# One-core attention and feed-forward layer: an unused load dropped, two weight loads moved ahead of two others, a bias product repeated, all engines' order rewritten

## Chip, core and metric

The kernel runs on one core of one Trainium2 chip. The metric is the device time of one execution in microseconds (us), the median of several runs. Before the change it is 332.9 us (three runs, 332.89 to 332.98).

## What is computed

The reference is one transformer layer on 256 tokens of width 1024 in float32. One wide projection is split into sixteen parts for four mixers; their outputs are joined, projected back, and followed by a feed-forward part.

```python
h = x @ w_in                                   # 256 x 1024 @ 1024 x 2956
(q_n, kc, vc, ks, vs, kw, vw, g_n, q_m, k_m, v_m, conv_in, q_h, f_h, i_h, g_h) = split(h)
kc = gelu(blocks(kc) @ w1[0] + b1[0]) @ w2[0]  # compressor, 15 blocks of 32 tokens; vc the same
o_nsa  = nsa_attention(q_n, kc, vc, ks, vs, kw, vw, sigmoid(g_n), rel_tab[:4])
o_moba = moba_attention(q_m, k_m, v_m, rel_tab[4:])
o_conv = silu(layer_norm(depthwise_conv31(a * sigmoid(g)) + b)) @ w_pw
o_hgrn = hgrn2(q_h, f_h, i_h, g_h)             # gated linear recurrence, chunks of 64
x = layer_norm(alpha * x + concat(o_nsa, o_moba, o_conv, o_hgrn) @ w_out)
x = layer_norm(alpha * x + square(relu(x @ w_ff1)) @ w_ff2)
```

## The kernel before

**Products.** Float32 products are made of parts: a weight is loaded raw, ScalarE rounds it to a high piece in the format fp32r (L245), VectorE subtracts to get the low piece (L246), and TensorE adds three products: high by high, high by low, low by high (L313 to L315, or L335 to L337 where the weight is the stationary side). The weights of ca, cg, qn and km are used raw in plain float32 (L310, L520). Names of the parts: ca and cg are the convolution's two inputs, n (n1) the keys and compressor inputs of NSA, qn its queries, ni (two halves, ni0 and ni1) the values, gates and HGRN's i, f, q and g those of HGRN, qm, km and vm those of MoBA, w1a and w1b the compressor's two weight matrices in two halves of 1 MB each.

**Loads.** SyncE's queue carries all weights, in the order of the list LOADS, into a pool `raws` of five slots of 1 MB. A transfer is issued when its slot is free, which is when the piece that was there has been rounded, subtracted or multiplied for the last time; behind it in the queue nothing is issued before. ScalarE's high pieces and VectorE's low pieces have three slots each (`his`, `los`), freed by the last product that reads them.

**Stages.** In order of time: the projections ca, cg, n, qn (8 to 33 us), ni (33.5 to 43.5), the compressor's products with w1a (L686), q and f together, score products of NSA (`tt` <- ksw, qn, L371) that VectorE empties with the bias table (L374) and ScalarE turns into weights p (L377, L388), transposes of p (L397), g, vm, qm, km, the four mixers, the product with w_out (L990 to L992) for two token tiles of 128, the first layer norm with its transposes by a product with a scaled identity (L1044, L1051), then the feed-forward part in sixteen groups, from about 146 us to the end. VectorE also does the convolution: 62 operations, one a tap and half (L571, L573), which stand wherever the order puts them, and HGRN's running sum, the scan (L616).

**First layer norm.** Each token tile t has two banks of transposed output, filled by a bias product (L1048, `acc` or `hg` <- bhot, bsum, 40 x 128 by 40 x 512) and four transposes each. The transposes wait for the tile's scale (L1044), at the end of a chain on VectorE that starts when w_out's banks of this tile are complete.

**Order.** Nothing is left to a scheduler at run time: the table ISSUE holds for PE, DVE, Activation, Pool and SP the order of every instruction, as indices into the program's own order, and `issue_in` makes each engine follow it. Each engine takes its instructions strictly in that order.

**Where the change touches it.** LOADS (L184), `load_w1` (L419 to L426), `tapw` (L488, L489), a tile in the space that `mixl` takes later, filled from the input `taps`; the branch CONV_T of `part_conv`, which does not run since CONV_T is empty; the bias product (L1048); ISSUE (L69 to L143).

Of the kernel before, what the change touches and what calls it, by code (L numbers as in the profile page):

```python
# [17 lines left out]
P = 128  # L18
S = 256
# [27 lines left out]
def shape_constants():  # L47
# [13 lines left out]
    for i, b in enumerate(LEVELS):  # L61
# [48 lines left out]
    ),  # L110
    DVE=(
# [13 lines left out]
    ),  # L125
    Activation=(
# [9 lines left out]
    ),  # L136
# [1080 lines left out]
```

## Time and profile before

| | |
|---|---|
| median of the runs | 332.9 us |
| profiled execution, its own time | 335.78 us |
| its span, from the first to the last instruction | 334.0 us |
| mean granted clock of TensorE | 0.986 |
| TensorE busy | 319.8 us (96%) |
| VectorE busy | 233.3 us (70%) |
| ScalarE busy | 166.8 us (50%) |

The profiled execution is 2.9 us above the median; the trace's times are those of this execution. PE is TensorE, DVE VectorE, ACT ScalarE, SP SyncE. A share over the whole span mixes the front (to 146 us, many short pieces on all engines) with the feed-forward part (TensorE in one stream). Where a wait ends is read from the timeline and the chain, and what cost a clock had from the windows.

### The profile page before, as it was taken

How to read it: one execution, taken by the hardware profiler on the slowest of the kernel's cores; microseconds unless marked ns; L12 is line 12 of the kernel's file. 1: busy time of each engine (PE TensorE's matmuls, PEld its weight loads, DVE VectorE, ACT ScalarE, POOL GpSimd, SP SyncE). 2: the span in 40 equal slices, each digit the busy share in tenths (PEclk: the TensorE clock that was granted, in tenths of full speed). 3: DMA queues.
4: the chain of work that ended last, by engine and by line, in shares of the span. 5: the costliest groups of instructions: out<-in, count | busy, mean ns of one | idle time of the engine just before them, and what ended most of it. 6: DMA issues, size and time to landing. Idle time of an engine off the chain costs nothing.

```text
span 334.0 us, 4992 instructions
## 1 busy us (share of the span) xinstructions
PE 319.8 (96%) x1929; PEld 273.1 (82%) x1929; DVE 233.3 (70%) x428; ACT 166.8 (50%) x307; POOL 10.5 (3%) x33
## 2 busy tenths in 40 slices
PE   8999969999999999989999999999999999999990
PEld 6897859898988778788888888888888888888880
DVE  0269969999989866886677477747564756568286
ACT  1464444784899982344365354535453545373100
POOL 3500000000000100000000000100000000000000
PEclk9999998999999999999999999999999999999996
DMA  7999799094300216556567555965565646520012
GB/s 234 387 398 416 235 395 388 15 371 135 121 0 2 54 74 251 153 226 186 214 232 251 176 203 155 318 202 207 153 226 160 219 144 233 156 98 0 2 49 77
DMA packets 18359, 62.75 MB, mean 188 GB/s; under 512 B 1784, under 2 KB 3664, under 8 KB 17696
## 3 DMA queue, kind: packets, MB, share of 16 engines
q1 hardware_dynamic: 15648, 56.61, 47.8%
q0 software_dynamic: 1056, 3.72, 3.2%
q10 hardware_dynamic: 1632, 2.11, 2.2%
q8 instruction: 15, 0.25, 0.3%
q14 instruction: 8, 0.07, 0.1%
HBM read 61.37 MB, written 1.06 MB: 187 GB/s over the span
## 4 chain that ended last, share of the span: by engine, by line
PE 86%; DVE 8%; DMA 2%; ACT 1%; issue 1%; DVEq 0%; ACTq 0%
PE mm L1102 15%; PE mm L1100 8%; PE hg L1121 5%; PE hg L1122 4%; PE tt L1122 4%; PE tt L1120 4%; PE hg L1120 4%; PE tt L1121 4%; DMA w_q_raw<-in_w_in_dram 2%; PE mm_km L310 2%; PE mm L1099 2%; PE mm_cg L310 2%; DVE yc L573 2%; PE acc L292 1%; PE tt L371 1%; PE tt L397 1%
## 5 line engine op out<-in xcount | busy, mean ns | idle before, releaser
L1102 PE MATMUL mm<-x1s,w_hi 128*128 128x512 f32 x210 | 74.4, 394 | 0.0
L246 DVE TENSOR_TENSOR r_lo<-r_raw,r_hi 128x1024 fp32r<-128x1024 f32 x40 | 47.4, 1221 | 24.8 <-ACT r_hi L245 24.8
L1100 PE MATMUL mm<-x1s,w_lo 128*128 128x256 f32 x240 | 61.0, 279 | 0.0
L245 ACT ACTIVATE r_hi<-r_raw 128x1024 fp32r<-128x1024 f32 x40 | 40.6, 1050 | 33.5 <-PE tt L1122 32.4
L1100 PEld LDWEIGHTS mm<-x1s,w_lo 128*128 128x128 f32 x240 | 44.9, 188 | 2.7
L1102 PEld LDWEIGHTS mm<-x1s,w_hi 128*128 128x128 f32 x210 | 39.2, 188 | 7.4
L246 DVE TENSOR_TENSOR w_lo<-w_raw,w_hi 128x1024 fp32r<-128x1024 f32 x32 | 37.8, 1218 | 5.0 <-ACT w_hi L245 5.0
L245 ACT ACTIVATE w_hi<-w_raw 128x1024 fp32r<-128x1024 f32 x32 | 32.2, 1051 | 4.6 <-DMA w_raw<-in_w_ff_dram 4.5
L1106 ACT ACTIVATE fx<-mm 128x256 f32<-128x256 f32 x30 | 11.4, 383 | 44.4 <-PE mm L1102 44.4
L1107 DVE TENSOR_TENSOR fs<-mm,fx 128x256 f32<-128x256 f32 x30 | 12.6, 424 | 28.5 <-ACT fx L1106 28.5
L573 DVE SCALAR_TENSOR_TENSOR yc<-hc,cols,yc 128x256 f32<-128x256 f32 x60 | 27.5, 479 | 0.5
L1121 PE MATMUL hg<-r_lo,fh 128*128 128x512 f32 (+1 forms) x70 | 26.4, 378 | 0.0
L1120 PE MATMUL hg<-r_hi,fh 128*128 128x512 f32 (+1 forms) x70 | 26.4, 377 | 0.0
L1121 PE MATMUL tt<-r_lo,fh 128*128 128x512 f32 x64 | 24.1, 396 | 0.0
L1122 PE MATMUL hg<-r_hi,fl 128*128 128x512 f32 (+1 forms) x70 | 22.4, 376 | 0.0
L1122 PE MATMUL tt<-r_hi,fl 128*128 128x512 f32 x64 | 20.8, 397 | 0.0
L1120 PE MATMUL tt<-r_hi,fh 128*128 128x512 f32 x64 | 20.8, 396 | 0.0
L1121 PEld LDWEIGHTS hg<-r_lo,fh 128*128 128x128 f32 x70 | 13.2, 189 | 2.7
L1122 PEld LDWEIGHTS hg<-r_hi,fl 128*128 128x128 f32 x70 | 13.2, 189 | 2.6
L1120 PEld LDWEIGHTS hg<-r_hi,fh 128*128 128x128 f32 x70 | 13.2, 188 | 2.1
L1121 PEld LDWEIGHTS tt<-r_lo,fh 128*128 128x128 f32 x64 | 12.1, 188 | 2.9
L1122 PEld LDWEIGHTS tt<-r_hi,fl 128*128 128x128 f32 x64 | 12.1, 189 | 2.8
(331 smaller groups left out, 650.7 us busy)
## 6 DMA issues: line engine op xcount, KB each, us to landing
w_raw<-in_w_ff_dram SPq DMA_DIRECT2D x32, 512.0 KB, 4.4
r_raw<-in_w_ff_dram SPq DMA_DIRECT2D x16, 1024.0 KB, 4.9
w<-in_nsa_cmp_w_dram SPq DMA_DIRECT2D x4, 1024.0 KB, 7.6
r_raw<-in_w_out_dram SPq DMA_DIRECT2D x4, 1024.0 KB, 6.1
w_ni_raw<-in_w_in_dram SPq DMA_DIRECT2D x2, 792.0 KB, 11.4
xf<-in_xt_dram ACTq DMA_DIRECT2D x4, 256.0 KB, 6.9
w_ca_raw<-in_w_in_dram SPq DMA_DIRECT2D x4, 256.0 KB, 7.1
w_cg_raw<-in_w_in_dram SPq DMA_DIRECT2D x2, 512.0 KB, 5.8
```

The lines of the kernel that those rows point to most:

```text
L245: A.activation(self.h[:, i:j], self.raw[:, i:j], AF.Copy)
L246: self.last = V.tensor_tensor(self.l[:, i:j], self.raw[:, i:j], self.h[:, i:j].bitcast(F32), op=ALU.subtract)
L310: T.matmul(dst[:, i], w.raw[:, k, P * i:P * i + P], xf[:, k], start=(k == 0), stop=(k == KT - 1))
L573: V.scalar_tensor_tensor(yc[:, i], h, w, yc[:, i], op0=ALU.mult, op1=ALU.add)
L1099: T.matmul(flat(pf[i]), h, flat(x1s[:, k]), start=True, stop=False)
L1100: T.matmul(pf[i][:, 0], l, x1h[:, k], start=False, stop=False)
L1102: T.matmul(flat(pf[i]), h, flat(x1s[:, k]), start=False, stop=(k == KT - 1))
L1106: A.activation(lo[:, i], pf[i][:, 1], AF.Copy)
L1107: V.tensor_tensor(sq[:, i], pf[i][:, 0], lo[:, i], op=ALU.add)
L1120: T.matmul(bank_, h, w.h[:, i, sl], start=(g == 0 and i == 0), stop=False)
L1121: T.matmul(bank_, h, w.l[:, i, sl], start=False, stop=False)
L1122: last = T.matmul(bank_, l, w.h[:, i, sl], start=False, stop=(g == NG - 1 and i == 1 and sl.stop != 768))
```

## The change

It does four things. The input `taps` and its load of 1 MB are dropped, with the branch that would have read it; the 62 taps on VectorE stay. In LOADS q stands before w1a and w1b before g, and w1a's first half goes to the space of `mixl` instead of a slot of `raws`; its load stands right behind qn's in SP's table. The last bias product (tile 1, second bank) is issued six times: five times as a product by itself, whose result the next overwrites, then as before. All five tables are new.

```diff
-    CONV_T = ()
-
-    LOADS = "ca cg n1 ni0 qn f ni1 qm w1a q km g w1b vm".split()
+    LOADS = "ca cg n1 ni0 qn f ni1 qm q w1a km w1b g vm".split()
...
         for i in range(2):
-            raw = raws.tile([P, 2048], F32, name="w1", tag="raw").rearrange("p (a b) -> p a b", a=8)
+
+            pool, tag = (raws, "raw") if c or i else (wk, "mixl")
+            raw = pool.tile([P, 2048], F32, name="w1", tag=tag).rearrange("p (a b) -> p a b", a=8)
             nc.sync.dma_start(raw, I["nsa_cmp_w1"][:, c, i])
...
-    tapw = wk.tile([P, 8, 8, 32], F32, name="tapw", tag="mixl")
-    late(tapw, I["taps"])
...
     def part_conv():
-        nonlocal pcv, yc
+        nonlocal yc
         at_(K["taps"])
         yc = t2_("c", "yc")
-        if CONV_T:
...
         for c in range(2):
-            T.matmul(pts[t][c], bsum, bhot[:, 4 * c:4 * c + 4, None].to_broadcast([40, 4, P]), start=True, stop=False)
+            to = pts[t][c], bsum, bhot[:, 4 * c:4 * c + 4, None].to_broadcast([40, 4, P])
+
+            for _ in range(5 if (t, c) == (1, 1) else 0):
+                T.matmul(*to, start=True, stop=True)
+            T.matmul(*to, start=True, stop=False)
...
     SP=(
-        "0-10 30 28-29 11-27 31-89 "
+        "0-10 18 30 28-29 11-17 19-27 31-89 "
     ),
```

What the tables do is seen in the order of the instructions. First SyncE's queue from f to vm (w_150 and w_152 are the halves of w1a, w_175 and w_177 those of w1b), before:

```order
L228 DMA w_f_raw<-in_w_in_dram 128x1024 x2
L228 DMA w_ni_raw<-in_w_in_dram 128x1584
L228 DMA w_qm_raw<-in_w_in_dram 128x1024 x2
L424 DMA w_150<-in_nsa_cmp_w_dram 128x2048
L424 DMA w_152<-in_nsa_cmp_w_dram 128x2048
L228 DMA w_q_raw<-in_w_in_dram 128x1024 x2
L228 DMA w_km_raw<-in_w_in_dram 128x1024 x2
L228 DMA w_g_raw<-in_w_in_dram 128x1024 x2
L424 DMA w_175<-in_nsa_cmp_w_dram 128x2048
L424 DMA w_177<-in_nsa_cmp_w_dram 128x2048
L228 DMA w_vm_raw<-in_w_in_dram 128x1024 x2
```

and after, from behind qn to w1b (w_159 and w_161 are the halves of w1a, w_166 and w_168 those of w1b):

```order
L424 DMA w_159<-in_nsa_cmp_w_dram 128x2048
L905 DMA pw<-in_conv_pw_w_dram 128x2x256
L665 DMA w_685<-in_nsa_cmp_w_dram 128x128
L667 DMA w2k<-in_nsa_cmp_w_dram 128x256
L226 DMA w_f_raw<-in_w_in_dram 128x1024 x2
L226 DMA w_ni_raw<-in_w_in_dram 128x1584
L226 DMA w_qm_raw<-in_w_in_dram 128x1024 x2
L226 DMA w_q_raw<-in_w_in_dram 128x1024 x2
L424 DMA w_161<-in_nsa_cmp_w_dram 128x2048
L226 DMA w_km_raw<-in_w_in_dram 128x1024 x2
L424 DMA w_166<-in_nsa_cmp_w_dram 128x2048
L424 DMA w_168<-in_nsa_cmp_w_dram 128x2048
```

w1a's first half went ahead of f, ni and qm, its second half behind q; w1b went ahead of g, which follows it, and vm follows g.

Next TensorE behind the last product of ni, where w1a's products (w_150 and w_152) end and those of q begin, before:

```order
L686 MATMUL acc<-w_150,blk_333 32x256
L686 MATMUL acc<-w_152,blk_334 32x256
L371 MATMUL tt<-ksw_329,qn 128x128
L371 MATMUL tt<-ksw_328,qn 128x128
L313 MATMUL mm_q<-xs,w_q_hi 128x256
L314 MATMUL mm_q<-xs,w_q_hi 128x256
L313 MATMUL mm_f<-xs,w_f_hi 128x256
L314 MATMUL mm_f<-xs,w_f_hi 128x256
L315 MATMUL mm_f<-xs,w_f_lo 128x256
```

and after (w_159 and w_161):

```order
L661 MATMUL acc<-w_159,blk_331 32x256
L661 MATMUL acc<-w_161,blk_332 32x256
L661 MATMUL acc<-w_159,blk_331 32x256
L311 MATMUL mm_q<-xs,w_q_hi 128x256
L311 MATMUL mm_f<-xs,w_f_hi 128x256
L312 MATMUL mm_f<-xs,w_f_hi 128x256
L313 MATMUL mm_f<-xs,w_f_lo 128x256
L311 MATMUL mm_f<-xs,w_f_hi 128x256
L312 MATMUL mm_f<-xs,w_f_hi 128x256
```

Both score products stood between w1a's last product and q; now they stand ahead of w1a's first, only nine of its sixteen products come before q, the other seven behind q and f, and a single product of q comes before f's.

Last TensorE at the end of w_out and the first layer norm (scale_1471 and scale_1498 are the scales of token tiles 0 and 1), before:

```order
L992 MATMUL tt<-r_hi,mixl 128x512
L1048 MATMUL acc<-bhot,bsum 128x512 x2
L1048 MATMUL hg<-bhot,bsum 128x512 x2
L1051 MATMUL acc<-scale_1471,x_1341 128x128 x4
L1051 MATMUL hg<-scale_1471,x_1341 128x128 x4
L1051 MATMUL hg<-scale_1498,x_1341 128x128 x4
```

and after (scale_1469 and scale_1496):

```order
L967 MATMUL tt<-r_hi,mixl 128x512
L1027 MATMUL hg<-bhot,bsum 128x512 x2
L1027 MATMUL acc<-bhot,bsum 128x512
L1026 MATMUL acc<-bhot,bsum 128x512 x5
L1027 MATMUL acc<-bhot,bsum 128x512
L1030 MATMUL hg<-scale_1469,x_1339 128x128 x4
L1030 MATMUL acc<-scale_1469,x_1339 128x128 x4
L1030 MATMUL hg<-scale_1496,x_1339 128x128 x4
```

The five extra products stand ahead of tile 0's transposes, with the other bias products; the banks are filled in the opposite order.

## Rows read from the trace of the kernel before

**Rows 1.** The page, part 4: shares of the chain that ended last.

```profile
PE 86%; DVE 8%; DMA 2%; ACT 1%; issue 1%; DVEq 0%; ACTq 0%
```

**Rows 2.** Waits of TensorE: us in total, times, longest.

```profile
PE mm_q L313 <- ACT iv L345: 2.6, 1, 2.6
```

**Rows 3.** Chain that ended last, around 40 us: start, us, what.

```profile
37.27 1.81 DVE w_ni_lo L246
39.10 7.20 DMA w_q_raw<-in_w_in_dram
46.40 1.06 ACT w_q_hi L245
```

**Rows 4.** TensorE's timeline: start, us, what, count [idle before <- releaser].

```profile
43.48 1.93 PE L686 MATMUL acc<-w,blk 128*32 128x256 f32 x32
...
48.39 0.57 PE L313 MATMUL mm_q<-xs,w_q_hi 128*128 128x256 f32 x1 [2.55 <-ACT iv L345]
...
52.04 0.28 PE L314 MATMUL mm_q<-xs,w_q_hi 128*128 128x256 f32 x1
...
52.99 0.28 PE L313 MATMUL mm_f<-xs,w_f_hi 128*128 128x256 f32 x1
```

**Rows 5.** 5 us windows: busy us (count) by engine, PEclk, DMA share, GB/s.

```profile
30.00:35.00 5.00, 4.31 (x22) 3.63 (x21) 4.86 (x13) 4.92 (x7) 0.00 (x0) 1.00 0.95 343
45.00:50.00 5.00, 2.45 (x19) 1.91 (x12) 2.48 (x11) 3.56 (x11) 0.00 (x0) 0.84 1.02 410
50.00:55.00 5.00, 5.00 (x36) 4.49 (x34) 4.39 (x13) 1.49 (x9) 0.00 (x0) 0.81 1.03 420
60.00:65.00 5.00, 5.00 (x61) 4.09 (x59) 4.64 (x13) 3.58 (x5) 0.00 (x0) 1.00 0.01 3
140.00:145.00 5.00, 3.70 (x25) 3.04 (x26) 4.68 (x13) 2.25 (x5) 0.00 (x0) 1.00 0.86 302
```

**Rows 6.** SyncE's queue: start of issue, us, what, count.

```profile
39.10 1.07 SPq L228 DMA_DIRECT2D w_q_raw<-in_w_in_dram  x2
...
52.20 0.80 SPq L228 DMA_DIRECT2D w_vm_raw<-in_w_in_dram  x2
```

**Rows 7.** DMA issues: count, KB each, median us to landing.

```profile
w_raw<-in_w_ff_dram SPq DMA_DIRECT2D x32, 512.0 KB, 4.4
...
tapw<-in_taps_dram POOLq DMA_DIRECT2D x1, 1024.0 KB, 11.2
...
w_km_raw<-in_w_in_dram SPq DMA_DIRECT2D x2, 512.0 KB, 8.6
...
w_vm_raw<-in_w_in_dram SPq DMA_DIRECT2D x2, 512.0 KB, 7.2
```

**Rows 8.** VectorE's timeline from 33 to 50 us.

```profile
33.45 0.41 DVE L595 TENSOR_TENSOR blk<-mm_n,cols 64x240 f32<-64x240 f32 x1
...
40.62 1.67 DVE L573 SCALAR_TENSOR_TENSOR yc<-hc,cols,yc 128x256 f32<-128x256 f32 x4
42.20 2.36 DVE L246 TENSOR_TENSOR w_qm_lo<-w_qm_raw,w_qm_hi 128x1024 fp32r<-128x1024 f32 x2
...
48.97 0.28 DVE L374 CUSTOM_DVE_ANT_0 p<-tt,toep 128x128 f32<-128x128 f32 x1
```

**Rows 9.** TensorE's timeline, first product of g.

```profile
65.15 0.39 PE L313 MATMUL mm_g<-xs,w_g_hi 128*128 128x256 f32 x1
```

**Rows 10.** ScalarE's timeline: the last scalings of p.

```profile
66.78 1.70 ACT L388 ACTIVATE p<-p,sm 128x256 f32<-128x256 f32 x4
```

**Rows 11.** TensorE's timeline at the first normalization.

```profile
139.88 0.70 PE L1048 MATMUL acc<-bhot,bsum 40*128 40x512 f32 x2
140.41 0.59 PE L1048 MATMUL hg<-bhot,bsum 40*128 40x512 f32 x2
141.05 1.16 PE L1051 MATMUL acc<-scale,x 128*128 128x128 f32 x8
...
144.36 1.16 PE L1051 MATMUL hg<-scale,x 128*128 128x128 f32 x8 [1.26 <-DVE scale L1044]
```

More of the change, by code (lines that the diff above doesn't have):

```diff
@@ L70 @@
     PE=(
[39 rows of a table removed]
[39 rows of a table added]
     ),
     DVE=(
[13 rows of a table removed]
[13 rows of a table added]
     ),
     Activation=(
[9 rows of a table removed]
[9 rows of a table added]
     ),
     Pool=(
-        "20-22 14 23-24 15 2 9-10 13 11-12 0-1 3-8 16-19 25-28 "
+        "19-21 13 22-23 14 2 8-9 12 10-11 0-1 3-7 15-18 24-27 "
     ),
     SP=(
-        "0-10 30 28-29 11-27 31-89 "
+        "0-10 18 30 28-29 11-17 19-27 31-89 "
     ),
@@ L539, in part_conv @@
     def part_conv():
-        nonlocal pcv, yc
+        nonlocal yc
         at_(K["taps"])
         yc = t2_("c", "yc")
-        if CONV_T:
-            W, H, n = 28 + S, 31 + S, len(CONV_T)
-            hc_d = dr.tile([P, n, H], F32, name="hc_d")
-            G.dma_start(hc_d, hc[:, CONV_T[0]:CONV_T[0] + n])
-            hcs = wk.tile([P, n, 4, W], F32, name="hcs", tag="hgw")
-            for i in range(n):
-                for j in range(4):
-                    G.dma_start(hcs[32 * j:32 * j + 32, i],
-                                bass.AP(tensor=hc_d.tensor, offset=hc_d.offset + i * H + j,
-                                        ap=[[n * H, 32], [32 * n * H, 4], [1, W]]))
-            pcv = hbank([P, n, S])
-            for i in range(n):
-                for b in range(8):
-                    for q in range(4):
-                        T.matmul(pcv[32 * q:32 * q + 32, i], tapw[:, 4 * CONV_T[i] + q, b], hcs[:, i, q, 4 * b:4 * b + S],
-                                 start=(b == 0), stop=(b == 7))
-            for i, c in enumerate(CONV_T):
-                A.activation(yc[:, c], pcv[:, i], AF.Identity, bias=cols[:, R_DB + c:R_DB + c + 1])
         at_(K["tapv"])
@@ L565, in part_conv @@
             for i in range(2):
-                if i in CONV_T:
-                    continue
                 w = cols[:, R_DW + 2 * k + i:R_DW + 2 * k + i + 1]
@@ L1181, in lay_out @@
                            for r, i, j in CHUNKS.values()], axis=1)
-    dw = a["conv_dw_w"][0]
-    taps = np.zeros((4, 32, 8, 8, 32), np.float32)
-    for k in range(31):
-        for c in range(32):
-            taps[(k + 1) % 4, c, :, (k + 1) // 4, c] = dw[k, c::32]
     brow = np.zeros((40, P), np.float32)
@@ L1192, in lay_out @@
     ff1 = a["w_ff1"][0].reshape(8, P, 16, 256).transpose(1, 2, 0, 3)
-    out = dict(x=a["x"], xt=tiles(a["x"][0].T), w_in=w_in, cols=rows.T, taps=taps.reshape(P, 8, 8, 32), brow=brow,
+    out = dict(x=a["x"], xt=tiles(a["x"][0].T), w_in=w_in, cols=rows.T, brow=brow,
                nsa_cmp_w1=w1, nsa_cmp_w2=w2, rel_bias=a["rel_bias"].T, w_ff1=ff1)
```

122 rows, old and new, of tables (Activation, DVE, PE) are left out of this document.

## Prediction

> **What bounds the kernel now.** I read the chain that ended last first: TensorE has 86% of it, VectorE 8%, a DMA 2% [rows 1]. So the time is TensorE's own work plus the places where it stands. The list of waits names the largest of these: 2.6 us, once, in front of the first product of q [rows 2]. The chain shows what it stood for: VectorE's low piece of ni's second half ends at 39.08, which frees a slot of the weight pool; only then is q's transfer issued, it needs 7.20 us, ScalarE rounds it in 1.06 [rows 3]. Read that way the label "ACT iv" in rows 2 is the last of a queue: ScalarE takes its work in order, so iv stood behind q's rounding, which stood for the DMA. SyncE's queue gives the same issue time, 39.10 [rows 6].
>
> TensorE's timeline there holds a second loss [rows 4]. After the idle 2.55 us, 17 products lie between 48.39 and 52.04, 0.215 us each; the next 8 take 0.95, 0.119 each. The windows say why: granted clock 0.84 and 0.81 in the two stretches, 1.00 in others [rows 5]. So the engine's clock fell to its lower level for part of them: 17 x 0.096 = 1.6 us, less the restart after the wait, call it 1.55. Two other idle times cost no clock: 0.69 in 30 to 35 and 1.26 at the first normalization, both at 1.00 [rows 5, 11].
>
> VectorE is the other thing to see. It is 97% busy in 30 to 35 and 93% in 60 to 65; only 45 to 50 has a hole, 2.5 us, the same stall [rows 5]. It can't give back much more than that.
>
> **The change, part by part.** The taps: one 1 MB transfer on POOL's queue, landing in 11.2 us [rows 7], gone, with nobody waiting for it. The first half of the compressor's weight w1a takes its place on SyncE's queue in size and nearly in time, so the sum of bytes up to 33 us stays. Gain 0; bounds 0 and the 0.69 idle of 30 to 35.
>
> The load order: q now stands ahead of w1a's second half and is released by the last product of ca, which the new order puts among n's products, near 25 us. Ahead of it in that queue are the same f, ni and qm as before. Issued 26 and given the slowest landing of its kind shown, 8.6 [rows 7], it is there by 35, long before ScalarE may round it. What is late next: q's rounded piece takes the slot of ni's, so it waits for ni's last product. That ended at 43.48 [rows 4]; one of the two score products inside ni has moved behind, 0.25, so about 43.2. Rounding 1.06 gives 44.3, the two copies of vn and iv behind it half a us more, 44.8. TensorE's own road to that place is shorter than before: a score product and nine of w1a's sixteen products, 0.25 + 9 x 0.12 = 1.3 (32 passes took 1.93 [rows 4]), so 44.5. The seven others come later, no work is lost. So of the stall of 2.55 some 0.3 stays, and the clock loss of 1.55 goes: -2.55 - 1.55 + 0.3 = **-3.8**.
>
> New waits. (a) The 21st product after that is a score product of 256 columns whose bank VectorE must have emptied. Counted along VectorE's new order from the end of the last block gather, 33.86 [rows 8]: two low pieces of f 2.4, a tap 0.4, ni's low piece 1.8 [rows 3], twelve taps 5.0 (four took 1.67), low pieces of qm and q with a tap between 2.8, two taps 0.8, two score operations 0.5 [rows 8] = 47.6. TensorE comes there at 44.8 + 20 x 0.119 = 47.2. **+0.4**, bounds 0 and 0.9. (b) g's products then start at 65.15 [rows 9] - 3.4 = 61.75; TensorE has done exactly the same work by then as before. g's low pieces on VectorE are due within a tap's length of that: **+0.2**, bounds 0 and 0.4. (c) vm is now released by the last use of w1a's second half, which has gone behind q and f: w1b's sixteen products (1.93) before g, 59.8 instead of 52.20 [rows 6]. Behind it on SyncE wait w_out and x, needed after 110 us, so that costs nothing. But ScalarE's new order puts vm's first rounding ahead of the last scalings of p, and TensorE wants those in the middle of g, after 27 products, four transposes and two small products: 61.75 + 0.2 + 3.5 = 65.4. The landing decides. vm itself took 7.2 at a DMA share of 1.03; at 60 to 65 the share was 0.01, the engines are free [rows 5, 7]. The nearest row is therefore that of the feed-forward's loads of the same size, 4.4: 59.8 + 4.4 + 1.06 + 0.43 for a scaling (four took 1.70 [rows 10]) = 65.7. **+0.3**; bounds 0 and, with 8.6, 4.5.
>
> The scan of HGRN and what hangs on it: five taps and vm's low piece now stand ahead of it on VectorE, so it comes no earlier than before, perhaps 3 us later in time. Its consumers on TensorE stand far behind g in either order. 0, bounds 0 and +1.
>
> The bias product: five more products, 0.265 each by the two pairs [rows 11] (0.235 in a stream). TensorE finished w_out at 139.88; four bias products, then token tile 0's transposes at 141.05, over at 143.10, then idle 1.26 until tile 1's scale, 144.36, so 4.48 after w_out. Now nine products 2.2 and the transposes 2.05: 4.25, if tile 1's scale comes earlier; the new order ends w_out with 28 products instead of 24 behind the bank that the normalization needs first, four products or 0.9 earlier. **-0.2**; bounds -0.7 and, if the scale is as late as ever and the transposes slip, +1.2.
>
> The feed-forward and the end have the same order, only numbered otherwise: 0.
>
> Sum: -3.8 + 0.4 + 0.2 + 0.3 - 0.2 = **-3.1**. The profiled execution took 335.78 with a span of 334.0; it would be 332.7 and 330.9. The median of the unprofiled runs is 332.9, 2.9 below the profiled one, and I take the difference over: **329.8**.
>
> **The rivals.**
>
> Full gain: the waits (a) to (c) don't come and the normalization gives 0.7: -3.8 - 0.7 = -4.5, **328.4**. For it: no wait above is over 0.4, all are differences of long sums.
>
> VectorE becomes the bound: it gets back only its hole of 2.5, and loses 1 of it where it now waits for score products and rounded pieces that come late in its fixed order. Then TensorE follows it: -1.5, **331.4**. For it 93 to 97% busy; against it, the taps among its work are wanted late, by the convolution's normalization, and were moved by the new order to fill holes.
>
> The clock stays low: 44.8 to 61 now has several short waits in place of a long one. The rows show the clock full across single idle times of 0.69 and 1.26 and low after 2.55; so I expect full. If it fell all the same, 1.55 comes back: **331.4**. The Trainium skill, page "TensorE: Matmul & The Clock Gate", section "A second HAM failure mode: psum-queue depth-cycling", says that frequent short idle times between groups of products can make the clock swing between its levels. By that rule this case would be the outcome; no run here shows it so far.
>
> Slower: vm's late load. Price and place as in (c): with km's landing of 8.6, 59.8 + 8.6 + 1.5 = 69.9 against 65.4, 4.5 instead of 0.3, in all +1.1: **334.0**. It decides from a landing of about 8.2 us on. For it: ScalarE in order, nothing to fill in; against it the empty queue at that time.
>
> No effect: q's transfer is early, but another operand holds the same place, as qm's pieces, iv or the score's bias table; or q's issue is late because its slot's release comes later than I read: 332.9.
>
> **How the numbers follow.** A measurement of this kernel can tell about 0.2% from no change, 0.67 us. Chances: forecast 0.50, full gain 0.14, VectorE 0.14, clock 0.06, slower 0.08, no effect 0.08. Faster: 0.50 + 0.14 + 0.14 + 0.06 = 0.84; same 0.08; slower 0.08. The range takes in the first four with their spread: 328.0 to 332.0; what is left out is 0.16.
>
> **What would show it.** Right: SyncE issues q before 30 us; no wait over 0.5 us in front of the first q product; granted clock 1.00 from 40 to 60; g's first product near 61.7; vm's issue near 59.8; TensorE's idle time in 44 to 66 about 1.2 in small pieces; 4.2 us from the end of w_out to tile 1's transposes. Wrong: a wait of over a us before a score product or a scaled p in 45 to 68, a clock under 0.9 there, or w_out ending later than 137.4 (139.88 less 2.9, with 0.4 to spare).

## The result, and the profile after

| | before | after |
|---|---|---|
| median | 332.89 us (332.21 to 332.98, 4 runs) | 334.8 us (334.7 to 335.61, 4 runs) |
| profiled execution | 335.78 us | 334.83 us |
| its span | 334.0 us | 333.1 us |
| mean granted clock | 0.986 | 0.993 |

After is to before as 1.0067, 95% interval 1.0047 to 1.0088: **slower by about 2.2 us** (1.9 by the medians), where 3.1 less was forecast. Yet the profiled execution of after is shorter than the one of before that the prediction was read from. Both things are true, and the first experiment says how.

The page of after, the engines' busy time and the chain that ended last (answers [rows 1]):

```profile
PE 321.4 (96%) x1934; PEld 273.0 (82%) x1934; DVE 234.4 (70%) x428; ACT 168.8 (51%) x307; POOL 10.0 (3%) x32
...
PE 85%; DVE 9%; DMA 2%; ACT 2%; issue 1%; ACTq 0%; DVEq 0%
```

Waits of TensorE, all that are listed: us in total, times, longest ([rows 2] had one of 2.6 before q):

```profile
PE acc L290 <- DVE idle L287: 1.2, 1, 1.2
PE mm_ni L333 <- DVE blk L570: 1.0, 1, 1.0
PE mm L517 <- DMA xf<-in_xt_dram: 0.5, 1, 0.5
PE mm L929 <- DVE yc L925: 0.3, 1, 0.3
PE mm L914 <- ACT ysq L911: 0.2, 1, 0.2
PE hg L843 <- DVE hgw L836: 0.2, 1, 0.2
```

Windows of 5 us of after (columns as in [rows 5]):

```profile
45.00:50.00 5.00, 5.00 (x42) 3.99 (x35) 3.87 (x15) 3.27 (x9) 0.00 (x0) 1.00 0.28 114
50.00:55.00 5.00, 5.00 (x40) 4.48 (x38) 5.00 (x15) 2.97 (x14) 0.00 (x0) 1.00 0.57 192
```

SyncE's queue in after (answers [rows 6]):

```profile
26.84 0.86 SPq L226 DMA_DIRECT2D w_q_raw<-in_w_in_dram  x2
...
61.08 0.80 SPq L226 DMA_DIRECT2D w_vm_raw<-in_w_in_dram  x2
```

So nearly all that was said of q came true: issued at 26.84, no wait in front of it, TensorE full and the clock 1.00 from 45 to 55. TensorE's timeline of after, at ni and q, the NSA scores of 256 columns, g, and the first normalization (answers [rows 4, 9, 11]):

```profile
34.39 0.42 PE L333 MATMUL mm_ni<-w_ni_hi,xs 128*128 128x396 f32 x1 [0.97 <-DVE blk L570]
...
45.77 0.38 PE L311 MATMUL mm_q<-xs,w_q_hi 128*128 128x256 f32 x1
...
48.35 0.70 PE L369 MATMUL tt<-ksw,qn 64*128 64x256 f32 x4
...
51.08 1.13 PE L369 MATMUL tt<-ksw,qn 64*128 64x256 f32 x6
...
62.68 0.39 PE L311 MATMUL mm_g<-xs,w_g_hi 128*128 128x256 f32 x1
...
139.49 0.70 PE L1027 MATMUL hg<-bhot,bsum 40*128 40x512 f32 x2
...
143.53 1.06 PE L1030 MATMUL hg<-scale,x 128*128 128x128 f32 x8
...
145.27 0.38 PE L1068 MATMUL mm<-x1s,w_hi 128*128 128x256 f32 x1
```

In [rows 11] the bias products began at 139.88; here they begin at 139.49. The stall of about 4 us is gone, and w_out ends only 0.4 earlier. Something took 3.7 us, of which 0.9 lie ahead of ni's first product: it starts at 34.39 here and at 33.53 in the profile of before:

```profile
33.53 0.45 PE L335 MATMUL mm_ni<-w_ni_hi,xs 128*128 128x396 f32 x1 [0.69 <-ACT qn L345]
```

### The profile page after: what moved, and what is told of

It reads as the page before. It is cut to its first block, busy times and chain, and to the rows that moved or that the text cites. A ratio compares the mean times of both kernels' runs of the same rounds, so it can differ in the third digit from the quotient of the medians.

```text
span 333.1 us, 5012 instructions
## 1 busy us (share of the span) xinstructions
PE 321.4 (96%) x1934; PEld 273.0 (82%) x1934; DVE 234.4 (70%) x428; ACT 168.8 (51%) x307; POOL 10.0 (3%) x32
## 3 DMA queue, kind: packets, MB, share of 16 engines
HBM read 60.32 MB, written 1.06 MB: 184 GB/s over the span
## 4 chain that ended last, share of the span: by engine, by line
PE 85%; DVE 9%; DMA 2%; ACT 2%; issue 1%; ACTq 0%; DVEq 0%
PE mm L1081 15%; PE mm L1079 8%; PE hg L1100 5%; PE hg L1101 5%; PE hg L1099 4%; PE tt L1101 4%; PE tt L1099 4%; PE tt L1100 4%; DMA xf<-in_xt_dram 2%; PE mm L1078 2%; PE mm_qn L308 2%; PE mm_cg L308 2%; PE acc L661 1%; PE mm L965 1%; PE tt L965 1%; PE mm L966 1%
## 5 line engine op out<-in xcount | busy, mean ns | idle before, releaser
L1086 DVE TENSOR_TENSOR fs<-mm,fx 128x256 f32<-128x256 f32 x30 | 12.6, 424 | 28.3 <-ACT fx L1085 28.3
```

Of the source, the lines that this page charges most:

```text
L1086: V.tensor_tensor(sq[:, i], pf[i][:, 0], lo[:, i], op=ALU.add)
```

## The experiments

### Is the stall of before there in other executions, and what are taps and bias worth?

Four kernels were run. Theory A: the profile of before caught an execution that is not the ordinary one. The rivals are that the taps, the early weight or the five bias products make the loss.

The kernel before, unchanged.

> The kernel before, unchanged, profiled once more. Theory A (the profile that I read was not typical: its execution took 335.78 us against a median of 332.9): this profile has no 2.55 us wait in front of q, or one under 1 us, no granted clock under 0.95 between 45 and 55 us, and a span near 331.1. Theory B (the stall is in every execution, and the 2.9 us lie outside the span): again a wait of about 2.5 us in front of q, clock 0.8 behind it, span near 334.

Measured: 332.36 us (12 runs), ratio 1.0003 (0.9992 to 1.0013); its profiled execution has a span of 330.9. Waits of TensorE, windows and ScalarE's rounding of q in it:

```profile
PE hg L1051 <- DVE scale L1044: 1.3, 1, 1.3
PE acc L292 <- DVE idle L289: 1.2, 1, 1.2
PE mm_ni L335 <- ACT qn L345: 0.7, 1, 0.7
PE mm_ni L336 <- DVE w_ni_lo L246: 0.2, 1, 0.2
```

```profile
45.00:50.00 5.00, 5.00 (x59) 4.12 (x52) 4.85 (x15) 4.63 (x18) 0.00 (x0) 1.00 1.02 388
50.00:55.00 5.00, 5.00 (x41) 4.49 (x41) 4.96 (x18) 1.28 (x5) 0.00 (x0) 1.00 1.01 417
```

```profile
44.58 1.06 ACT L245 ACTIVATE w_q_hi<-w_q_raw 128x1024 fp32r<-128x1024 f32 x1 [2.64 <-PE mm_ni L337]
```

The same landmarks of TensorE's timeline in it, and the four scores of 256 columns that come after q's first product:

```profile
34.51 0.45 PE L335 MATMUL mm_ni<-w_ni_hi,xs 128*128 128x396 f32 x1 [0.69 <-ACT qn L345]
...
50.77 1.14 PE L371 MATMUL tt<-ksw,qn 64*128 64x256 f32 x8
...
62.00 0.39 PE L313 MATMUL mm_g<-xs,w_g_hi 128*128 128x256 f32 x1
...
136.77 0.70 PE L1048 MATMUL acc<-bhot,bsum 40*128 40x512 f32 x2
...
143.10 0.39 PE L1089 MATMUL mm<-x1s,w_hi 128*128 128x256 f32 x1
```

There is no wait in front of q and no low clock. q is issued at 40.08, even later than the 39.10 of [rows 6], but lands in time: its two transfers take 4.5 us in the median here and 7.6 in the execution read before. ScalarE waits for the last product of ni, a slot, not for the transfer.

From ni's first product to g's first it takes 27.5 us here and took 65.15 - 33.53 = 31.6 in the execution read before: 4.1 more, the price that the prediction gave the stall with its clock. The whole span is only 3.1 longer, since ni begins 1.0 later here (34.51).

Of the 93 executions of before in all these experiments (81 beside them, 12 of e1) 92 lie between 331.5 and 333.3 us; one has 335.79 us, span 334.0, clock 0.987. By these numbers it is the twin of the one the prediction read (335.78, 334.0, 0.986); a trace of it was not kept. **The stall and the low clock are not in the ordinary execution; one in some ninety has a time like that.** Theory A holds. Why the transfer took longer in that execution stays open.

Before, without the taps and with the first half of w1a loaded early in a tile of its own:

```diff
-            raw = raws.tile([P, 2048], F32, name="w1", tag="raw")...
+            pool, tag = (raws, "raw") if c or i else (wk, "mixl")
+            raw = pool.tile([P, 2048], F32, name="w1", tag=tag)...
-    late(tapw, I["taps"])
```

> The kernel before, with its order of all engines, but the taps not loaded, and w1a's first half loaded right behind qn into the space of mixl; so q's transfer is released by qn's last product near 33 us instead of by ni's low piece at 39.1. Theory A (ordinary executions of before hardly stall): 332.9, within 0.7. Theory B (the stall is in every execution): q's wait goes, 332.9 - 2.5 - 1.5 = about 329.

Measured: 332.69, ratio 1.0000 (0.9987 to 1.0013). Worth nothing, as forecast.

After, with the last bias product once (the five repeats taken out of program and table):

```diff
-            for _ in range(5 if (t, c) == (1, 1) else 0):
-                T.matmul(*to, start=True, stop=True)
```

> The changed kernel with the last bias product issued once instead of six times, all else in its order. Theory A (the five products push tile 0's transposes behind its scale, and tile 1's scale is there before they end): 0.4 faster than the changed kernel, 334.4. Theory B (they keep the clock up through the normalization): slower than the changed kernel, 335.5 or more, with a granted clock under 1.00 behind 140 us.

Measured: 334.66, ratio to before 1.0069 (1.0055 to 1.0082), 0.14 less than after by the medians, where theory A expected 0.4; theory B (335.5 or more, a lower clock) is out, the granted clock from 140 to 145 us is 1.00. Its wait for tile 1's scale is 0.5 where before has 1.3, and from its first bias product to the feed-forward it takes 5.4 us, where after takes 5.8. So in the new order the repeats fill 0.5 of waiting and add some 0.35, too little for these few runs to tell.

Before, with the five repeats put in at the same place.

> The kernel before with the last bias product issued six times, behind the other three, all else as it was. Theory A (they fill the idle 1.26 us in front of tile 1's transposes): 332.9, within 0.3; tile 0's transposes start 1.1 us later, tile 1's at the same distance from w_out's end as before. Theory B (tile 1's chain on VectorE hangs on tile 0's transposes): about 1.1 us slower, 334.0.

Measured: 332.19, ratio 0.9993 (0.998 to 1.0005); the wait for the scale falls from 1.3 to 0.3. In the order of before the five products stand in time that was idle: they cost nothing and gain nothing.

So the 2.2 us are in neither of the small parts. Set against the ordinary execution of before, e1's, after's profile is longer by 2.2 (333.1 against 330.9), and the landmarks divide it: from ni's first product to g's first, 28.3 against 27.5, +0.8; from there to the first bias product, 76.8 against 74.8, +2.0; from there to the feed-forward, 5.8 against 6.3, -0.55. Apart from the repeats, the products are the same in number. In the middle part some 0.7 us are the three last waits in after's list, and the half-array products take 1.1 more. In the first part the scores take 0.6 more: before has four of 256 columns in a row (50.77), after one of them beside one of 128 columns (48.35) and three by themselves (51.08), and the three take as long as the four did. The compressor's products take 0.4 more there, and the 0.2 that e1 waits inside ni is gone.

### The order of the instructions or the order of the loads?

The changed kernel's loads with the tables of before, and the other way round (the program's own order of the three engines' instructions is the same in both, so the tables can be exchanged; only the repeats are left out):

```diff
-    PE=( the changed kernel's ), DVE=( ... ), Activation=( ... )
+    PE=( before's ), DVE=( ... ), Activation=( ... )
```

> The changed kernel (taps gone, q and the compressor's weight loaded ahead of g and vm, last bias product once) with the kernel before's tables for TensorE, VectorE and ScalarE; only SP's and POOL's tables stay the new ones. Theory T (the new order of instructions costs the 2 us): 332.5 us, between 332.0 and 333.0, the same as before. Rival L (the new order of loads costs it: g 0.9 us and vm later than before): 334.7, as the changed kernel with the bias once.

Measured: 332.14, ratio 0.9995 (0.9983 to 1.0007). The new loads with the old order are as fast as before. **The loss is in the new order of instructions.**

> The kernel before, its loads, their order and the taps kept, with the changed kernel's tables for TensorE, VectorE and ScalarE (last bias product once). Theory T: 334.7 us, or above where the new order wants q earlier than it lands. Rival L: 332.6, no change.

Measured: 341.37, ratio 1.0275 (1.0261 to 1.0289), far over both expectations, by a wait that neither named: 4.9 us of TensorE for a transfer of w1b. The new order's use of w1a is too late for the old loads; the next kernel shows how. This run doesn't weigh T against L.

### The parted groups

The theory G looks at products that fill only a part of the array: the compressor's (32 wide) in fours, the 64 x 64 and 64 x 128 ones in pairs. Four groups of them stand whole in the old order and parted in the new one. (A fifth, the scores of 256 columns behind q's first product, is parted in the new order too; these runs left it whole.) First the groups were parted in before:

```diff
-296-311 362-363 ... 312-327
+296-304 362-363 ... 305-327
-488-495 404-411 334-337 412 444 496-497 445-447 498-499 413-415 544 416 545 417
+488-494 404-406 495 407-411 334-337 412 444-447 413-414 496-497 415 544 416 545 498-499 417
```

> The kernel before with four groups of narrow products on TensorE parted as in the changed kernel, nothing else moved: the compressor's 16 products of 32 rows' width as 9 and 7, the eight 64x64 products as 7 and 1, and the group of eight half-array products (four scores with four of hg) as four scores and two pairs apart. Theory G (products that use different parts of the array run side by side only within an unbroken group): +0.4 us for the first, +1.1 for the others, 334.1 us. Rival W (only waits cost; narrow products take the same time wherever they stand): 332.6.

Measured: 342.06, ratio 1.0293 (1.0275 to 1.0311), 8 us over what G expected. SyncE's queue, the wait, and the window after it:

```profile
49.98 11.03 SPq L427 DMA_DIRECT2D w<-in_nsa_cmp_w_dram  x2
```

```profile
PE acc L689 <- DMA w<-in_nsa_cmp_w_dram: 4.8, 1, 4.8
```

```profile
65.00:70.00 5.00, 4.52 (x38) 2.44 (x39) 0.00 (x0) 0.84 (x2) 0.00 (x0) 0.66 0.98 400
```

In before w1b's transfers need the slots of w1a, and their queue entries go through at 46.47 in 0.86 us (e1). The seven products that I put behind q and f hold w1a's slots; the second of w1b's two transfers is now held until they are done, TensorE stands 4.8 us, and the granted clock of the window in which it starts again is 0.66. My edit moved a release, and I had priced only the products. e6 has the same wait. In the changed kernel it does not come: the first half of w1a has a tile of its own, w1b's two transfers are issued at 38.78 and 51.17, before the seven products (59.96), and only vm's waits for them (61.08).

So the same parting went into e5's kernel, which has those loads.

> The kernel of e5 (new loads, old order, 332.1 us) with the same groups of narrow products parted as in e7: the compressor's 16 as 9 and 7, the eight 64x64 products as 7 and 1, the mixed group of eight half-array products as four scores and two pairs. Here the compressor's first weight is loaded early into a tile of its own, so no later load hangs on its last product and the stall of e7 should not come. Theory G (the parted groups cost time as such): +0.4 and +1.1, 333.6 us. Rival W (they are made up for at the next wait, and only waits count): 332.1. In the trace either way: the parted groups should take about 0.4 and 1.1 us more of TensorE's time than in e5.

Measured: 334.28 (334.11 to 335.29, 6 runs), ratio to before 1.0068 (1.005 to 1.0085), where e5 has 0.9995. **With the groups parted the old order is as slow as the changed kernel (1.0067).** TensorE's timeline of e5, groups whole:

```profile
43.72 1.94 PE L665 MATMUL acc<-w,blk 128*32 128x256 f32 x32
45.59 0.49 PE L373 MATMUL tt<-ksw,qn 64*128 64x128 f32 x4
...
79.04 0.28 PE L316 MATMUL mm_qm<-xs,w_qm_hi 128*128 128x256 f32 x1
79.16 0.28 PE L317 MATMUL mm_qm<-xs,w_qm_lo 128*128 128x256 f32 x1
79.37 0.68 PE L811 MATMUL hg<-dd 64*64 64x64 f32 x16
79.98 0.39 PE L315 MATMUL mm_qm<-xs,w_qm_hi 128*128 128x256 f32 x1
80.20 0.28 PE L316 MATMUL mm_qm<-xs,w_qm_hi 128*128 128x256 f32 x1
...
82.14 0.48 PE L373 MATMUL tt<-ksw,qn 64*128 64x256 f32 x1
...
83.66 0.39 PE L315 MATMUL mm_qm<-xs,w_qm_hi 128*128 128x256 f32 x1
```

and of e9, parted:

```profile
43.65 1.48 PE L666 MATMUL acc<-w,blk 128*32 128x256 f32 x18
45.06 0.49 PE L374 MATMUL tt<-ksw,qn 64*128 64x128 f32 x4
...
59.17 2.79 PE L666 MATMUL acc<-w,blk 128*32 128x256 f32 x46
61.89 0.39 PE L316 MATMUL mm_g<-xs,w_g_hi 128*128 128x256 f32 x1
...
81.15 0.32 PE L812 MATMUL hg<-dd 64*64 64x64 f32 x2
81.41 0.39 PE L316 MATMUL mm_qm<-xs,w_qm_hi 128*128 128x256 f32 x1
...
83.21 1.14 PE L374 MATMUL tt<-ksw,qn 64*128 64x256 f32 x8
84.27 0.39 PE L316 MATMUL mm_qm<-xs,w_qm_hi 128*128 128x256 f32 x1
...
84.70 0.71 PE L823 MATMUL hg<-de 64*128 64x128 f32 x4
85.34 0.39 PE L318 MATMUL mm_qm<-xs,w_qm_lo 128*128 128x256 f32 x1
...
86.01 0.71 PE L823 MATMUL hg<-de 64*128 64x128 f32 x4
86.65 0.39 PE L317 MATMUL mm_qm<-xs,w_qm_hi 128*128 128x256 f32 x1
```

Read from start to start, since ends overlap. The mixed group of scores and hg products takes 83.66 - 82.14 = 1.52 in one piece, and 1.06 + 0.64 + 0.64 = 2.34 in three. The compressor's passes (two a product) take 45.59 - 43.72 = 1.87 for 32, twice; as 18 and 46 they take 1.41 + 2.72 = 4.13, 0.4 more. The starts of the single passes, read from the trace, tell why: four products run side by side, their first passes 7 ns apart, their second passes 0.2 us later, then the next four. Sixteen and sixteen are eight fours, 16 steps; 9 is 4 + 4 + 1 and 23 is five fours and 3, nine sets, 18 steps: two more of 0.2. The lone product of hg<-dd takes 0.26, one in the whole group of eight 0.61 / 8 = 0.08; the other seven still take 0.60, so it adds 0.25. And each change of kind delays its neighbour: a full product before a group is followed 0.21 later instead of 0.12 (79.16 and 79.04), and the first full product after one takes 0.22 (79.98 to 80.20). Together 0.82 + 0.40 + 0.25 = 1.5 us, as G expected of the groups. The run lost more than G's 1.5: the neighbours (some 0.7) and a wait of 0.2 before q make up the rest of the 2.3 by which e9's span exceeds e5's (332.4 against 330.1). None of it is idle time, except that 0.2: the page counts it as work, and TensorE's busy time reads 320.3 us in e9 and 318.2 in e5.

The Trainium skill, page "TensorEngine Tiling (Array Packing)", section "Key Properties", says that a change of the tiling mode drains TensorE. The extra 0.1 us on either side of a narrow group agrees with it, though the trace does not show the drain itself.

Then the reverse, after with the groups joined where nothing they need comes later:

```diff
-296-304 152 ... 305-327
+152 ... 296-327
-488-490 492 491 494 493 409-410 551 411-413 495-497 414
+488-495 409-410 551 411-413 414
-424 498-499 425
+424 496 498 497 499 425
```

> The changed kernel with the bias once, with the same groups joined again where nothing that they need comes later: the compressor's products as 16, the 64x64 products as eight in a row, the four hg products of the next step in one group at the later of their two places (scores stay alone). Theory G: 0.4 + 0.25 + 0.6 less than the 334.7 of the changed kernel with the bias once, so 333.4 us, less what ScalarE loses by the first two of the four coming some 2.3 us later (up to +0.5). Rival W: 334.7, or more by that wait.

Measured: 335.54, ratio 1.0097 (1.0083 to 1.0112), 0.9 more than e3 instead of 1.3 less. The groups did shrink, by 0.55 (compressor) and 0.49 (hg) from start to start. But:

```profile
PE mm_q L314 <- ACT w_q_hi L246: 0.7, 1, 0.7
PE hg L846 <- DVE hgw L839: 0.5, 2, 0.3
```

These two waits give back most of the 1.0 that the groups won. Of the 0.9 by which the span is longer than e3's (333.7 against 332.8), 0.4 lie ahead of ni's first product, where both kernels have the same order; and the full products of q, f and vm take some 0.7 more, which no run here explains.

The compressor's nine products had covered the time until q's high piece was rounded, and the hg products now wait 0.5 for hgw, 0.2 in after. Within this order the parting has its use, and taking it back alone, as in e8, did not pay. The order buys a TensorE without a gap at q with narrow groups in pieces, and in the ordinary execution of before there was no gap at q.

### A version that beats both

e5's list shows 1.2 us in front of ni, for the last of VectorE's four blk operations. The table has three convolution taps right ahead of them and a fourth among them. Put behind:

```diff
-37 39-41 25-27 43 28 42 44 8 46 45 47 10
+37 25-28 39-41 43 42 44 8 46 45 47 10
```

> The kernel of e5 with one thing moved on VectorE: the four products that form blk (they free the bank that ni's first product waits for) go three steps of the depthwise convolution earlier, some 1.5 us. In e5 ni's first product waits 1.2 us for the last of them. If TensorE's time after ni carries through, as the account of e5 and the changed kernel says (almost no idle time behind ni), the wait goes and the kernel ends 0.8 to 1.2 us earlier, 331.1. Rival: the wait turns up again at the next operand that VectorE or ScalarE makes (ni's second half, q, f), and the time stays 332.1.

Measured: 332.26, ratio 1.0001 (0.9988 to 1.0014). The rival was right; TensorE's waits:

```profile
PE mm_ni L338 <- DVE w_ni_lo L248: 1.3, 1, 1.3
```

Then that low piece, of ni's second half, went ahead of the three taps before it too (`44 8 10 46 45 47`).

> The kernel of e10 with the next operand moved too: on VectorE the low half of ni's second weight goes three steps of the convolution earlier (some 1.3 us), the place where e10's wait of 1.3 us turned up. If that was the whole of the second wait, ni starts about 1.1 us earlier than in e5 and stays without a wait, and what follows up to the first layer's end moves with it: 331.1 us against 332.1 to 332.4 for e5 and before. Rival (a chain of loads and ScalarE behind it keeps the place of q): the wait turns up once more at q or f, and the time stays 332.2.

Measured: 331.82 (331.13 to 332.64, 12 runs), ratio 0.9978 (0.9965 to 0.9991): 0.7 us less than before, faster than both kernels, though by less than the 1.1 expected, and with an interval that is close to 1. No wait at ni is left; 0.2 before q and the 1.3 for tile 1's scale remain, besides the one at the start. The profiled execution is one of the slowest of the twelve (332.62), so no trace shows where the 0.7 was won.

## Why the prediction was wrong

**The base.** The step that failed first is the last one of the sum: the median is "2.9 below the profiled one, and I take the difference over". The 2.9 were the stall, less the 1.0 by which that execution was earlier at ni. Of the -3.8 for q (2.55 of wait, 1.55 of clock, 0.3 left) the ordinary execution of before has nothing to give: no wait at q, clock 1.00 (e1). The numbers for it were on the table: a profiled execution 2.9 us above three runs that agree within 0.1, with a stall and clock loss of 4.1 that hung on how fast one transfer landed. (That the three agreed so closely was chance: 92 later executions spread over 1.8 us.) Taken as it stood against its own time, the sum of -3.1 gave 332.7 for that execution; after took 334.83. So of the 5.0 by which the forecast of 329.8 missed the measured 334.8, 2.9 are the base. The other 2.1 are the next step: ni's later start in after (0.9) and the waits (a) to (c) that did not come (0.9) cancel.

**The order.** The second is "the seven others come later, no work is lost". Work was lost, 0.4 us by the 9 and 7 and 1.1 by the half-array groups, with more at their neighbours (e9), and 0.6 by the parted scores (read from the traces alone). I costed the new table by counts of products and by waits, and read product durations of narrow groups as if they held wherever the product stands. No rival of the five had this mechanism. That it is the order and not the loads is shown by e5; that partings alone make a loss of this size, by e9. That they make all of after's loss is not shown: e9 left the scores whole, e8 did not win the loss back, and the three small waits of after between 98 and 110 us, 0.7 in all, were not tried by themselves. Read from the traces, 0.4 + 1.1 + 0.6 + 0.7 less the 0.55 won at the normalization is 2.25, against 2.2 in the spans; what else differs, the neighbours too, nearly cancels.

**q's own steps** were right: issue before 30 (26.84), no wait over 0.5, clock 1.00. q's first product was put at about 44.8 and came at 45.77; g's at 61.75, and it came at 62.68. Both come 0.9 late because ni does: it began at 34.39, and at 33.53 in the profile that the prediction reckoned from. From ni's first product to g's first, 28.2 was said and 28.3 came, by luck: the 0.3 left before q and wait (a)'s 0.4 did not come, and the partings, priced at nothing, took their place.

**New waits** (a) score bank +0.4, (b) g's low pieces +0.2, (c) vm +0.3: none came; TensorE was full from 45 to 55 and 60 to 65, where 1.2 us of idle time in small pieces had been said for 44 to 66. vm was issued at 61.08 (said 59.8) and landed in 4.1 us, the nearer of the two rows taken. The rival of vm's late load is out, and with it the one place from which "slower" was expected.

**Full gain**: its conditions came, no wait (a) to (c) and a gain of about 0.5 at the normalization, but not its 328.4, since both steps above were wrong in it too. **VectorE as the bound**: no wait of after's list between 35 and 95 us names it; the one ahead of that, 1.0 for blk before ni, stands where before has 0.7 for ScalarE's qn. **The low clock**: 1.00 in both windows. The rule on frequent short idle times was not put to the test, since there were none from 45 to 55 us.

**Taps**: 0, as said (e2). **Normalization**: said 4.2 us from the end of w_out to tile 1's transposes, found 143.53 - 139.49 = 4.04, against 4.48 in before; -0.2 was said, -0.55 up to the feed-forward was found. The repeats did not win it (e4: no gain in the old order; e3: without them the same stretch is 5.4 instead of 5.8); what came earlier is tile 1's scale (e3: a wait of 0.5 instead of 1.3).

The mark for "wrong" that the prediction gave, w_out ending later than 137.4, is what came: 139.49.

## What to carry to other kernels

Where the profiled execution and the median of the runs differ by more than the runs among themselves, first ask which stall of the profile could be that difference; if it is not in the ordinary run, it can't be won there. When an order is costed, products that use a part of the array have no duration of their own: count unbroken groups, fours and pairs, and the changes between full and narrow products. A moved product also moves the release of what it reads, so look at which transfer waits for that slot.

## What was not expected of the hardware

Narrow products side by side: four of the compressor's, 32 wide, start 7 ns apart, and a lone one takes the same steps of 0.2 us as four. Scores and hg products of different halves mixed in one group took 1.52 us, and apart 2.34 (e5, e9). Each change between full and narrow products cost about 0.1 us on either side. The same transfer of q, issued at nearly the same time, landed in 4.5 us in one execution and 7.6 in another of the same kernel. In the window of 5 us in which TensorE starts again after a wait of 4.8 us the granted clock was 0.66 (e7), after 2.55 us 0.84 and 0.81 ([rows 5]); in the windows around waits of up to 1.3 it was 1.00.
